# Output projection of a hybrid encoder layer: the second norm one slot later, transposes three tiles behind, attention outputs and denominators loaded two tiles at a time

## The chip, the cores and the metric

One Trainium2 chip (trn2); the kernel is one program on 1 core. The metric is device microseconds of one execution, lower is better. Where the text says "before", it is the kernel ahead of the change.

## The reference, cut to what matters

One encoder layer on x of 2048 positions by 1024 channels, in float32. The part around the change is the end of the mixing sub-layer and the start of the MLP:

```python
attn = dilated_attention(q, k, v, rel_bias).reshape(B, S, D_ATTN)          # 8 heads x 64
sgu = spatial_gating(jax.nn.gelu(zu), jax.nn.gelu(zv), ...)                # 512 channels
mix = jnp.concatenate([attn, sgu], axis=-1) @ w_out                        # (2048 x 1024) @ (1024 x 1024)
x = x + rms_norm(mix, g_post_mix)                                          # first norm
h = rms_norm(x, g_pre_ffn)                                                 # second norm
f = jnp.square(jax.nn.relu(h @ w_ff1)) @ w_ff2                             # hidden width 4096
return x + rms_norm(f, g_post_ffn)
```

The attention output of a head is a sum over three branches divided by a common denominator. The kernel stores the undivided sum and the reciprocal of the denominator, and multiplies the two when the output projection loads them.

## The kernel before, in words

Every matrix product is made of three passes (`mm3`, lines 90 to 94): each float32 operand is split into a high half, rounded to float32r, and the rest, and high times low, low times high and high times high are summed in PSUM. So a product of a 128-position tile with 512 output columns over 128 input channels is three matmuls of 128x512.

The program has three stages. Stage 1 (line 158) makes q, k, v and the gate's inputs. Stage 2 (line 387) does the attention head by head; between its steps a filler, `gate` (line 665), makes the spatial gating unit, and then the half of the output projection that belongs to the gate's 512 channels: its tiles `ot` go to the DRAM tensor `part` (2048 x 1024). The attention sums go to the DRAM tensor `od` (512 channels x 2048 positions) and the reciprocal denominators to `rd` (8 heads x 2048). Stage 3 (line 880) adds the attention half of the projection to `part`, does both norms, and then runs the MLP in two halves of 1024 positions.

The change is in stage 3's first loop (lines 953 to 1025), the output projection. It has 18 slots, `i` = 0 to 17, and works on tiles of 128 positions. In slot `i` before the change:

- `halves(i + 1)` (line 971): ScalarE casts the tile `fa` (attention output, already multiplied) to its high half `mh`, VectorE makes the rest `ml` (lines 59 and 60).
- Loads, all issued from SyncE's queue: `load_x(i)` (the residual, line 963, 3 buffers), `load_part(i + 1)` (line 957, 4 buffers, tile `r`), and `load_attn(i + 3)` (line 863): two DMAs for the denominators `fd`, each broadcasting the rows of 4 heads over 64 partitions, and one for `fa`. `fd` lies in the buffers `g` and `fs` in turn, one buffer each; `fa` in one of three `fr`.
- TensorE: 24 matmuls of 128x512 for the tile, in two halves `n` of 512 columns; in slots 7 to 9 and 11 to 14 also the steps of two early units of the MLP's first product (`early`, line 983; a step is 6 matmuls of 128x512, 16 steps in all; the ninth step of a unit is its end, where ScalarE, GpSimd and VectorE make `sq`, its square and the split `fh`, `fl`, lines 938 to 947).
- The first norm of tile `i - 1`: `meansq` (line 897) is a pass of ScalarE that squares and sums `r` (`jk`), then two small GpSimd instructions give `rs`; VectorE multiplies `r` by `rs` and the gain (line 1009) and adds the residual (line 1010).
- The result is stored to `x1d` by a DMA issued from ScalarE's own queue (line 1012), and for the first 8 tiles the second norm follows at once: `normed` (line 905) is another `meansq` of the same tile and a ScalarE pass that scales it into the residual's buffer `xt` (line 907).
- VectorE adds the PSUM banks `mo` to `r` (line 1016), one for each half.
- `turned(i - 2)` (line 909): 8 TensorE transposes of 128x128, two ScalarE casts `hh`, two VectorE subtractions `hl`.
- `product(i + 2)` (line 875): GpSimd multiplies `fa` by `fd`.
- In slots 1 to 4 two weight pieces `wraw` of the MLP are loaded; in slots 2 to 5 the two of the slot before are split into `wh` and `wl` (lines 56 and 57).

Tile 0's attention load and product stand at the end of stage 2 (lines 855 and 856), tile 1's and 2's loads at the head of stage 3. The order in which these lines stand is the order of execution on each engine: at the end of the loop `in_order` (line 35) chains all instructions of TensorE, ScalarE, VectorE, GpSimd and SyncE in program order. So an instruction that waits holds back all that follows it on its engine, and a DMA that waits for its buffer holds back all later DMAs of its queue.

```python
   985	                if i + 1 < 16:
   986	                    halves(i + 1)
...
  1007	                    if old and n == 0:
  1008	                        rs = meansq(r)
...
  1013	                        if i - 1 < 8:
  1014	                            normed(r, xt)
...
  1017	                if 0 <= i - 2 < 8:
  1018	                    turned(xs[i - 2], h[0], h[1], i - 2)
  1019	                if i + 2 < 16:
  1020	                    product(nc, c, i + 2)
```

Of the kernel before, what the change touches and what calls it, by code (L numbers as in the profile page):

```python
# [9 lines left out]
F32 = mybir.dt.float32  # L10
F32R = mybir.dt.float32r
BF16 = mybir.dt.bfloat16
AF = mybir.ActivationFunctionType
ALU = mybir.AluOpType
# [3 lines left out]
P = 128  # L18
# [3 lines left out]
DH = 64  # L22
# [30 lines left out]
def split_sbuf(nc, src, hi, lo, scale=None):  # L53

    if scale is not None:
        nc.scalar.activation(hi, src, AF.Copy, scale=scale)  # L56
        nc.vector.scalar_tensor_tensor(lo, src, scale, f32(hi), ALU.mult, ALU.subtract)  # L57
        return
    nc.scalar.copy(hi, src)  # L59
    nc.vector.tensor_tensor(lo, src, f32(hi), ALU.subtract)  # L60
# [326 lines left out]
def stage2(tc, c, a):  # L387
    nc = tc.nc
    LEAD = 2
    with ExitStack() as ctx:  # L390
# [386 lines left out]
        for s_ in range(NH * NG):  # L777
            g = s_ % NG
# [73 lines left out]
            for run in jobs.pop(min(jobs)):  # L852
                run()
        c.loads = {}
        load_attn(nc, c, 0)
        product(nc, c, 0)
        for _ in fill:
            pass
# [1 line left out]

def load_attn(nc, c, i):

    sl = slice(i * P, (i + 1) * P)
    fa = c.fk.tile([P, 4, P], F32, name="fa", tag="fr", bufs=3)
    fr = c.fk.tile([P, 512], F32, name="fd", tag=("g", "fs")[i % 2], bufs=1).rearrange("p (k s) -> p k s", k=4)
    rv = c.rd[:, sl].rearrange("(k e) s -> e k s", e=2)
    for e in range(2):
        nc.sync.dma_start(fr[e * DH:(e + 1) * DH], rv[e].partition_broadcast(DH))  # L870
    nc.sync.dma_start(fa, c.od[:, sl].rearrange("(k p) s -> p k s", p=P))
    c.loads[i] = fa, fr


def product(nc, c, i):
    fa, fr = c.loads[i]
    nc.gpsimd.tensor_tensor(fa, fa, fr, ALU.mult)


def stage3(tc, c, a, out):  # L880
    nc = tc.nc
# [3 lines left out]
    with ExitStack() as ctx:  # L885
# [11 lines left out]
        def meansq(src):  # L897
            jk = wk.tile([P, 512], F32, name="jk3", tag="sq").bitcast(BF16)
            ms = sm.tile([P, 1], F32, name="ms3", tag="ms3")
            nc.scalar.activation(jk, src, AF.Square, scale=1.0 / 32.0, accum_out=ms)  # L900
            rs = sm.tile([P, 1], F32, name="rs3", tag="rs3")
            rstd_pow(nc, rs, ms, RMS_EPS, c)
            return rs

        def normed(x1, out):
            rs = meansq(x1)
            nc.scalar.activation(out, x1, AF.Copy, scale=rs)

        def turned(x1, hh, hl, i):
            for j in range(2):  # L910
                t = pt.tile([P, 512], F32, name="tp3", tag="tp3")
                for k in range(4):
                    kc = 4 * j + k
                    nc.tensor.transpose(t[:, k * P:(k + 1) * P], x1[:, kc * P:(kc + 1) * P], c.ident)
                split_psum(nc, t.rearrange("p (k t) -> p k t", k=4), hh[:, 4 * j:4 * j + 4, i * P:(i + 1) * P],
                           hl[:, 4 * j:4 * j + 4, i * P:(i + 1) * P])
# [6 lines left out]
        h = new_h()  # L923
# [29 lines left out]
        with ExitStack() as octx:  # L953
            orp = octx.enter_context(tc.tile_pool(name="s3r", bufs=4, side="right"))
            gmix = bcast_row(nc, cst, a["g_post_mix"][0:1], D, "gmix", "gain")

            def load_part(i):

                r = orp.tile([P, D], F32, name="r", tag="r")
                nc.sync.dma_start(r, c.part[i * P:(i + 1) * P, :])  # L960
                return r

            def load_x(i):
                xt = wk.tile([P, D], F32, name="xt3", tag="xt3", bufs=3)
                nc.sync.dma_start(xt, x2[i * P:(i + 1) * P, :])
                return xt

            start = len(nc.cur_bb.bb.instructions)
            parts, xs, ops = {}, {}, {}

            def halves(i):
                mh = c.fk.tile([P, 4, P], F32R, name="mh", tag="xh", bufs=2)
                ml = c.fk.tile([P, 4, P], F32R, name="ml", tag="xl", bufs=2)
                split_sbuf(nc, c.loads.pop(i)[0], mh, ml)
                ops[i] = mh, ml

            load_attn(nc, c, 1)
            parts[0] = load_part(0)
            halves(0)
            load_attn(nc, c, 2)  # L980
            product(nc, c, 1)
            raws, ws0, fs0, fs1 = [], [], [], []
            early = {7: 3, 8: 3, 9: 3, 11: 3, 12: 2, 13: 2, 14: 2}
            for i in range(18):
                if i + 1 < 16:
                    halves(i + 1)
                if i < 16:
                    xs[i] = load_x(i)
                if i + 1 < 16:
                    parts[i + 1] = load_part(i + 1)  # L990
                if i + 3 < 16:
                    load_attn(nc, c, i + 3)
                if i in (7, 11):
                    unit = ff1_unit(h, ws0, 0, (i // 11,), fs0, fpa)
                old = 0 <= i - 1 < 16
                if old:
                    r, xt = parts[i - 1], xs[i - 1]
                for n in range(2):
                    if i < 16:
                        b = pm.tile([P, 512], F32, name="mo", tag="mm3")  # L1000
                        ns = slice(n * 512, (n + 1) * 512)
                        mh, ml = ops[i]
                        for kc in range(4):
                            mm3(nc, b, mh[:, kc, :], ml[:, kc, :], *c.wo[4 * n + kc], kc == 0, kc == 3)
                    for _ in range((early.get(i, 0) + 1 - n) // 2):
                        next(unit, None)
                    if old and n == 0:
                        rs = meansq(r)
                        nc.vector.scalar_tensor_tensor(r, r, rs, gmix, ALU.mult, ALU.mult)
                        nc.vector.tensor_tensor(r, r, xt, ALU.add)  # L1010
                    if old and n == 1:
                        nc.scalar.dma_start(x1d[(i - 1) // 8][((i - 1) % 8) * P:((i - 1) % 8 + 1) * P, :], r)
                        if i - 1 < 8:
                            normed(r, xt)
                    if i < 16:
                        nc.vector.tensor_tensor(parts[i][:, ns], b, parts[i][:, ns], ALU.add)
                if 0 <= i - 2 < 8:
                    turned(xs[i - 2], h[0], h[1], i - 2)
                if i + 2 < 16:
                    product(nc, c, i + 2)  # L1020
                for _ in range(len(raws)):
                    ws0.append(piece_split(nc, c, raws.pop(0), c.gffn[:, len(ws0):len(ws0) + 1]))
                if 1 <= i < 5:
                    raws = [piece_load(nc, c, w1[kc * P:(kc + 1) * P, 0:512]) for kc in range(2 * i - 2, 2 * i)]
            in_order(tc, start, ("PE", "Activation", "DVE", "Pool", "SP"))
# [194 lines left out]
```

## Time and profile before

| | us |
|---|---|
| three runs | 2499.51, 2507.77, 2511.3 |
| their median | 2507.77 |
| the profiled execution's own time | 2505.61 |
| its span, first to last instruction | 2503.8 |
| TensorE busy in the span | 2391.6 (96%) |
| output projection, first to last `mo` matmul | 954.7 to 1108.8 |

All times in the rows below are microseconds from the start of the span of that one profiled execution, unless marked ns. TensorE (PE) is busy nearly everywhere, but its matmuls are pipelined and a busy TensorE may run at a lower clock: the column PEclk gives the clock that was granted, as a share of 2.4 GHz. DVE is VectorE, ACT ScalarE, POOL GpSimd; SPq and ACTq are the DMA queues of SyncE and ScalarE. "Idle before" an instruction is how long its engine stood idle ahead of it, with what ended the wait.

### The profile page before, as it was taken

What the parts mean: (1) busy time and instruction counts of PE and PEld (TensorE: products, weight loads), DVE (VectorE), ACT (ScalarE), POOL (GpSimd) and SP (SyncE); (2) the same over time, 40 slices, a digit from 0 to 9 for tenths busy, and PEclk for the clock granted to TensorE, in tenths of its full rate; (3) what the DMA queues carried; (4) which work ended last, traced back from release to release, by engine and by line L of the source; (5) the groups of instructions that cost most, each with busy time, mean ns of one, the idle gap of its engine ahead of it and who ended that gap; (6) DMA issues with size and microseconds to landing.
All of it is one profiled execution on the core that took longest, in us unless ns stands there. A gap on an engine that the chain in (4) does not pass through costs nothing.

```text
span 2503.8 us, 31495 instructions
## 1 busy us (share of the span) xinstructions
PE 2391.6 (96%) x11591; PEld 1994.1 (80%) x11591; DVE 1063.0 (42%) x2246; ACT 930.8 (37%) x2053; POOL 459.3 (18%) x521
## 2 busy tenths in 40 slices
PE   7999999989888887999999999999999999999998
PEld 6787888878777776778888888888788888888887
DVE  5534523667766643651323332332722233233326
ACT  4424422467766662523221221123533122212212
POOL 4103103633222222320110010011211001001101
PEclk9999999999899998999999999999999999999999
DMA  7736365877776556872111211111611111111113
GB/s 270 221 134 202 135 187 164 223 183 184 190 184 160 144 156 184 234 242 68 51 51 34 67 46 48 43 51 59 211 51 51 40 62 48 49 39 54 48 47 118
DMA packets 222078, 296.14 MB, mean 118 GB/s; under 512 B 37089, under 2 KB 128740, under 8 KB 218852
## 3 DMA queue, kind: packets, MB, share of 16 engines
q1 hardware_dynamic: 214404, 272.62, 36.8%
q10 hardware_dynamic: 4960, 17.31, 1.8%
q0 software_dynamic: 2560, 4.20, 1.2%
q8 instruction: 91, 1.49, 0.2%
q14 instruction: 63, 0.52, 0.1%
HBM read 216.04 MB, written 82.74 MB: 119 GB/s over the span
## 4 chain that ended last, share of the span: by engine, by line
PE 60%; DMA 9%; DVE 4%; ACT 3%; POOL 2%; issue 1%; SPq 1%; ACTq 0%; DVEq 0%; POOLq 0%
PE f L92 10%; PE f L93 10%; PE f L94 10%; PE g L92 8%; PE g L94 8%; PE g L93 8%; DMA fa<-od 2%; DMA v<-vd 2%; PE t L595 1%; PE o L623 1%; PE o L624 1%; PE s L515 1%; ACT p L584 1%; PE s L516 1%; DMA x1b<-stb 1%
## 5 line engine op out<-in xcount | busy, mean ns | idle before, releaser
L92 PE MATMUL g<-wl,fh 128*128 128x512 f32 x1024 | 399.1, 390 | 0.4 <-ACT sq L945 0.4
L94 PE MATMUL g<-wh,fh 128*128 128x512 f32 x1024 | 398.8, 389 | 0.0
L93 PE MATMUL g<-wh,fl 128*128 128x512 f32 x1024 | 398.7, 389 | 0.0
L94 PE MATMUL f<-hh,wh 128*128 128x512 f32 x1024 | 398.7, 389 | 0.0
L93 PE MATMUL f<-hh,wl 128*128 128x512 f32 x1024 | 398.7, 389 | 0.0
L92 PE MATMUL f<-hl,wh 128*128 128x512 f32 x1024 | 398.5, 389 | 0.0
L946 POOL TENSOR_TENSOR sq<-sq 128x512 f32<-128x512 f32 x128 | 134.0, 1066 | 1150.7 <-ACT sq L945 1150.7
L56 ACT ACTIVATE wh<-wraw,gain 128x512 fp32r<-128x512 f32 x200 | 143.2, 724 | 504.0 <-PE g L94 423.3
L57 DVE SCALAR_TENSOR_TENSOR wl<-wraw,gain,wh 128x512 fp32r<-128x512 f32 x200 | 157.9, 797 | 265.1 <-ACT wh L56 264.4
L60 DVE TENSOR_TENSOR fl<-sq,fh 128x512 fp32r<-128x512 f32 x128 | 100.3, 783 | 383.4 <-ACT fh L59 372.8
L92 PEld LDWEIGHTS g<-wl,fh 128*128 128x128 f32 x1024 | 192.3, 188 | 40.4 <-ACT sq L945 0.8
L93 PEld LDWEIGHTS f<-hh,wl 128*128 128x128 f32 x1024 | 192.2, 188 | 40.1
L92 PEld LDWEIGHTS f<-hl,wh 128*128 128x128 f32 x1024 | 192.2, 188 | 40.1
L94 PEld LDWEIGHTS f<-hh,wh 128*128 128x128 f32 x1024 | 192.2, 188 | 39.9
L94 PEld LDWEIGHTS g<-wh,fh 128*128 128x128 f32 x1024 | 192.2, 188 | 39.8
L93 PEld LDWEIGHTS g<-wh,fl 128*128 128x128 f32 x1024 | 192.3, 188 | 39.6
L1073 DVE TENSOR_TENSOR acc<-g,acc 128x512 f32<-128x512 f32 x192 | 127.2, 687 | 165.1 <-PE g L94 165.1
L584 ACT ACTIVATE p<-p,m 128x256 f32<-128x256 f32 (+2 forms) x384 | 174.1, 459 | 18.8 <-DVE m L556 18.8
L945 ACT ACTIVATE sq<-f 128x512 f32<-128x512 f32 x128 | 74.6, 597 | 281.0 <-PE f L94 274.3
L60 DVE TENSOR_TENSOR wl<-wraw,wh 128x512 fp32r<-128x512 f32 x136 | 93.8, 690 | 165.9 <-ACT wh L59 164.6
L59 ACT CAST wh<-wraw 128x512 fp32r<-128x512 f32 x136 | 84.5, 622 | 183.2 <-PE f L94 162.4
L532 DVE CUSTOM_DVE_ANT_0 p<-s,bias 128x256 f32<-128x256 f32 (+2 forms) x384 | 121.1, 355 | 39.1 <-PE s L516 25.4
(166 smaller groups left out, 4158.5 us busy)
## 6 DMA issues: line engine op xcount, KB each, us to landing
wraw<-in_w_ff_dram SPq DMA_DIRECT2D x256, 256.0 KB, 2.7
wraw<-in_w_in_dram SPq DMA_DIRECT2D x72, 256.0 KB, 2.8
xt<-in_x_dram SPq DMA_DIRECT2D x32, 512.0 KB, 6.6
v<-vd SPq DMA_DIRECT2D x40, 256.0 KB, 6.4
v<-vd SPq DMA_DIRECT2D x8, 1088.0 KB, 7.7
hd<-ht ACTq DMA_DIRECT2D x16, 512.0 KB, 4.6
vd<-vt SPq DMA_DIRECT2D x16, 512.0 KB, 3.3
qd<-e SPq DMA_DIRECT2D x32, 256.0 KB, 2.8
```

Of the source, the lines that this page charges most:

```text
L56: nc.scalar.activation(hi, src, AF.Copy, scale=scale)
L57: nc.vector.scalar_tensor_tensor(lo, src, scale, f32(hi), ALU.mult, ALU.subtract)
L59: nc.scalar.copy(hi, src)
L60: nc.vector.tensor_tensor(lo, src, f32(hi), ALU.subtract)
L92: nc.tensor.matmul(out, lhsT=lh, rhs=rl, start=start, stop=False)
L93: nc.tensor.matmul(out, lhsT=ll, rhs=rh, start=False, stop=False)
L94: nc.tensor.matmul(out, lhsT=lh, rhs=rh, start=False, stop=stop)
L532: nc.vector.tensor_tensor_reduce(po, so, bo, -1.0, 1e38, ALU.add, ALU.min, o.nm[:, br, cc:cc + 1])
L584: nc.scalar.activation(p[:, at + lo:at + hi], p[:, at + lo:at + hi], AF.Exp, bias=o.m[:, br, cc:cc + 1], scale=-1.0, accum_out=o.dn[:, br, ...
L945: nc.scalar.activation(sq, bs[k * len(es) + e], AF.Relu)
L946: nc.gpsimd.tensor_tensor(sq, sq, sq, ALU.mult)
L1073: nc.vector.tensor_tensor(av, b, av, ALU.add)
```

## The change

- The second norm of a tile moves one slot later: in slot `i` `meansq` runs for tile `i - 2` (second norm) and then for tile `i - 1` (first norm), both ahead of the slot's matmuls in program order; the scaling into `xt` is for tile `i - 2`.
- The store to `x1d` moves to the next slot and from ScalarE's queue to SyncE's, at the head of the slot's loads.
- `turned` works on tile `i - 3` and moves from the end of the slot to its start, ahead of the tile's matmuls.
- `load_attn` loads two tiles (256 positions) at once, in even slots. It is cut by channels instead: for each half of the channels (4 heads) two denominator DMAs and one of the outputs, so that `fa` and `fd` are two tiles of 128x512 each. The numbers and sizes of the DMAs for two tiles stay (4 of 128 KB and 2 of 256 KB), their contiguous pieces grow from 512 B to 1 KB. `fd` lies in `g` and `fs`, both used by each pair; the first pair's lie in stage 2's pool `p`. `fa` lies in `fr`, for odd pairs the second half in `fu`.
- `product` multiplies both halves of a pair, in even slots; the load of the next pair stands right behind it. `halves` splits a tile in two pieces of 128x256.

```diff
@@ -852,7 +852,7 @@
             for run in jobs.pop(min(jobs)):
                 run()
         c.loads = {}
-        load_attn(nc, c, 0)
+        load_attn(nc, c, 0, pp)
         product(nc, c, 0)
         for _ in fill:
             pass
@@ -860,21 +860,26 @@
 
 
 
-def load_attn(nc, c, i):
-
-    sl = slice(i * P, (i + 1) * P)
-    fa = c.fk.tile([P, 4, P], F32, name="fa", tag="fr", bufs=3)
-    fr = c.fk.tile([P, 512], F32, name="fd", tag=("g", "fs")[i % 2], bufs=1).rearrange("p (k s) -> p k s", k=4)
-    rv = c.rd[:, sl].rearrange("(k e) s -> e k s", e=2)
-    for e in range(2):
-        nc.sync.dma_start(fr[e * DH:(e + 1) * DH], rv[e].partition_broadcast(DH))
-    nc.sync.dma_start(fa, c.od[:, sl].rearrange("(k p) s -> p k s", p=P))
-    c.loads[i] = fa, fr
+def load_attn(nc, c, i, pool=None):
+
+    sl = slice(2 * i * P, 2 * i * P + 2 * P)
+    fa, fd = [], []
+    for j in range(2):
+        fa.append(c.fk.tile([P, 512], F32, name="fa", tag=("fr", ("fr", "fu")[i % 2])[j],
+                            bufs=(3, (3, 1)[i % 2])[j]).rearrange("p (k s) -> p k s", k=2))
+        d = pool.tile([P, 512], F32, name="fd", tag="p") if pool else \
+            c.fk.tile([P, 512], F32, name="fd", tag=("g", "fs")[j], bufs=1)
+        fd.append(d.rearrange("p (k s) -> p k s", k=2))
+        rv = c.rd[4 * j:4 * j + 4, sl].rearrange("(k e) s -> e k s", e=2)
+        for e in range(2):
+            nc.sync.dma_start(fd[j][e * DH:(e + 1) * DH], rv[e].partition_broadcast(DH))
+        nc.sync.dma_start(fa[j], c.od[2 * j * P:2 * j * P + 2 * P, sl].rearrange("(k p) s -> p k s", p=P))
+    c.loads[i] = fa, fd
 
 
 def product(nc, c, i):
-    fa, fr = c.loads[i]
-    nc.gpsimd.tensor_tensor(fa, fa, fr, ALU.mult)
+    for fa, fd in zip(*c.loads[i]):
+        nc.gpsimd.tensor_tensor(fa, fa, fd, ALU.mult)
 
 
 def stage3(tc, c, a, out):
@@ -971,30 +976,33 @@
             def halves(i):
                 mh = c.fk.tile([P, 4, P], F32R, name="mh", tag="xh", bufs=2)
                 ml = c.fk.tile([P, 4, P], F32R, name="ml", tag="xl", bufs=2)
-                split_sbuf(nc, c.loads.pop(i)[0], mh, ml)
+                for j, fa in enumerate(c.loads[i // 2][0]):
+                    split_sbuf(nc, fa[:, :, i % 2 * P:i % 2 * P + P], mh[:, 2 * j:2 * j + 2, :], ml[:, 2 * j:2 * j + 2, :])
                 ops[i] = mh, ml
 
             load_attn(nc, c, 1)
             parts[0] = load_part(0)
             halves(0)
-            load_attn(nc, c, 2)
-            product(nc, c, 1)
             raws, ws0, fs0, fs1 = [], [], [], []
             early = {7: 3, 8: 3, 9: 3, 11: 3, 12: 2, 13: 2, 14: 2}
             for i in range(18):
+                old = 0 <= i - 1 < 16
+                if 0 <= i - 3 < 8:
+                    turned(xs[i - 3], h[0], h[1], i - 3)
                 if i + 1 < 16:
                     halves(i + 1)
+                if 0 <= i - 2 < 16:
+                    nc.sync.dma_start(x1d[(i - 2) // 8][((i - 2) % 8) * P:((i - 2) % 8 + 1) * P, :], parts[i - 2])
+                    if i - 2 < 8:
+                        rs2 = meansq(parts[i - 2])
+                if old:
+                    rs = meansq(parts[i - 1])
                 if i < 16:
                     xs[i] = load_x(i)
                 if i + 1 < 16:
                     parts[i + 1] = load_part(i + 1)
-                if i + 3 < 16:
-                    load_attn(nc, c, i + 3)
                 if i in (7, 11):
                     unit = ff1_unit(h, ws0, 0, (i // 11,), fs0, fpa)
-                old = 0 <= i - 1 < 16
-                if old:
-                    r, xt = parts[i - 1], xs[i - 1]
                 for n in range(2):
                     if i < 16:
                         b = pm.tile([P, 512], F32, name="mo", tag="mm3")
@@ -1005,19 +1013,17 @@
                     for _ in range((early.get(i, 0) + 1 - n) // 2):
                         next(unit, None)
                     if old and n == 0:
-                        rs = meansq(r)
+                        r = parts[i - 1]
                         nc.vector.scalar_tensor_tensor(r, r, rs, gmix, ALU.mult, ALU.mult)
-                        nc.vector.tensor_tensor(r, r, xt, ALU.add)
-                    if old and n == 1:
-                        nc.scalar.dma_start(x1d[(i - 1) // 8][((i - 1) % 8) * P:((i - 1) % 8 + 1) * P, :], r)
-                        if i - 1 < 8:
-                            normed(r, xt)
+                        nc.vector.tensor_tensor(r, r, xs[i - 1], ALU.add)
+                    if 0 <= i - 2 < 8 and n == 1:
+                        nc.scalar.activation(xs[i - 2], parts[i - 2], AF.Copy, scale=rs2)
                     if i < 16:
                         nc.vector.tensor_tensor(parts[i][:, ns], b, parts[i][:, ns], ALU.add)
-                if 0 <= i - 2 < 8:
-                    turned(xs[i - 2], h[0], h[1], i - 2)
-                if i + 2 < 16:
-                    product(nc, c, i + 2)
+                if i % 2 == 0 and i + 2 < 16:
+                    product(nc, c, i // 2 + 1)
+                    if i + 4 < 16:
+                        load_attn(nc, c, i // 2 + 2)
                 for _ in range(len(raws)):
                     ws0.append(piece_split(nc, c, raws.pop(0), c.gffn[:, len(ws0):len(ws0) + 1]))
                 if 1 <= i < 5:
```

## Rows read from the trace of the kernel before

**Rows 1.** Windows: PE, PEld, DVE, ACT, POOL busy us, PEclk, DMA share, GB/s

```profile
960.00:970.00 10.00, 2.03 (x6) 1.07 (x5) 1.56 (x3) 0.62 (x1) 1.26 (x1) 0.63 0.84 174
970.00:1028.00 58.00, 48.42 (x182) 36.41 (x181) 31.84 (x42) 28.54 (x47) 15.45 (x26) 0.83 0.78 231
1006.00:1017.00 11.00, 8.67 (x33) 6.35 (x32) 6.94 (x11) 6.07 (x11) 2.83 (x5) 0.84 0.69 218
1028.00:1058.00 30.00, 29.24 (x135) 23.75 (x135) 17.57 (x23) 15.17 (x26) 8.54 (x15) 1.00 0.87 250
1072.00:1109.00 37.00, 37.00 (x162) 30.18 (x161) 19.59 (x22) 8.83 (x16) 10.95 (x14) 1.00 0.70 232
```

**Rows 2.** TensorE's waits, 954 to 1122: us in total, times, longest us

```profile
PE mo L92 <- ACT mh L59: 9.7, 5, 8.0
PE mo L93 <- DVE ml L60: 3.1, 4, 1.8
PE tp L914 <- DVE hl L84: 6.3, 4, 3.2
PE tp L914 <- ACT xt L907: 1.8, 1, 1.8
```

**Rows 3.** Timeline of SyncE's queue and of GpSimd: start, us, instruction, idle before

```profile
956.96 0.57 SPq L871 DMA_DIRECT2D fa<-od  x1
...
966.50 1.26 POOL L877 TENSOR_TENSOR fa<-fa,fd 128x512 f32<-128x512 f32 x1 [15.64 <-DMA fa<-od]
```

**Rows 4.** Timeline of ScalarE, slots 1 to 6

```profile
974.66 0.62 ACT L59 CAST mh<-fa 128x512 fp32r<-128x512 f32 x1 [6.25 <-POOL fa L877]
...
1005.67 0.61 ACT L59 CAST mh<-fa 128x512 fp32r<-128x512 f32 x1
...
1011.27 1.06 ACT L900 ACTIVATE jk<-r 128x1024 bf16<-128x1024 f32 x1 [3.94 <-DVE r L1010]
...
1013.42 1.15 ACT L907 ACTIVATE xt<-r,rs 128x1024 f32<-128x1024 f32 x1 [0.99 <-POOL rs L99]
...
1027.63 0.61 ACT L59 CAST mh<-fa 128x512 fp32r<-128x512 f32 x1
```

**Rows 5.** Timeline of TensorE: tile 0, then transposes and tile 7

```profile
957.83 0.39 PE L93 MATMUL mo<-qs,ml 128*128 128x512 f32 x1
...
960.10 0.39 PE L94 MATMUL mo<-ks,mh 128*128 128x512 f32 x1
...
1026.80 1.25 PE L914 MATMUL tp<-ident,xt 128*128 128x128 f32 x8 [0.32 <-DVE hl L84]
1028.30 0.51 PE L92 MATMUL mo<-qs,mh 128*128 128x512 f32 x1 [0.25 <-ACT mh L59]
```

**Rows 6.** VectorE's groups by shape, 880 to 1130: busy us, mean ns, idle before

```profile
L60 DVE TENSOR_TENSOR ml<-fa,mh 128x512 fp32r<-128x512 f32 x16 | 11.0, 687 | 46.3 <-ACT mh L59 46.3
```

**Rows 7.** DMA queues and issues, 954 to 1037: KB each, median us to landing

```profile
q1 hardware_dynamic: 12853, 14.94, 66.2%
q10 hardware_dynamic: 833, 3.05, 9.1%
...
r<-part SPq DMA_DIRECT2D x9, 512.0 KB, 7.4
xt<-in_x_dram SPq DMA_DIRECT2D x8, 512.0 KB, 13.0
x1d<-r ACTq DMA_DIRECT2D x6, 512.0 KB, 9.6
fd<-rd SPq DMA_DIRECT2D x18, 128.0 KB, 11.9
...
wraw<-in_w_ff_dram SPq DMA_DIRECT2D x9, 256.0 KB, 10.1
```

**Rows 8.** Timeline of ScalarE in slot 9, end of the first early unit

```profile
1058.51 0.59 ACT L945 ACTIVATE sq<-f 128x512 f32<-128x512 f32 x1
...
1063.85 0.63 ACT L59 CAST fh<-sq 128x512 fp32r<-128x512 f32 x1 [2.12 <-POOL sq L946]
```

## The prediction

> **What bounds the kernel now.** I read the page first, where TensorE is busy nearly throughout, so only stretches in which it waits or runs slow can give time. The windows show where the change's stretch is of that kind: from 960 to 970 it works 2.03 of 10 us at a clock of 0.63, from 970 to 1028 it works 48.42 of 58 us at 0.83, and from 1072 to 1109 it works 37.00 of 37 at full clock [rows 1]. So the output projection loses time in its first seven tiles and next to none later, where the early MLP steps fill TensorE. How much there is to win: the waits of TensorE in the stretch add up to 9.7 + 3.1 + 6.3 + 1.8 = 20.9 us [rows 2], and the lower clock costs about 2.03 x 0.37 + 48.42 x 0.17 = 9.0 us [rows 1]. The ceiling is some 30 us, 1.2% of the time. A difference under 0.5% (12.5 us) can't be told from none here.
>
> What it waits for is read from two timelines. The longest wait is tile 1: GpSimd stood idle 15.64 us before its product at 966.50, because `fa` was issued only at 956.96 [rows 3]. After it each slot is paced by ScalarE. In slot 4 it casts `mh` at 1005.67, squares tile 3, and then, at 1011.27, it has stood idle 3.94 us before the second square of the same tile, which needs VectorE's multiply and add, and 0.99 us for the root [rows 4]; `mh` of slots 1 and 6 stand at 974.66 and 1027.63, so five slots take 53.0 us, 10.6 each. The scaled `xt`, the transposes and the next slot's `mh` all queue behind that. TensorE sees the end of it.
>
> **The change, part by part.** All is summed against the profiled execution, 2505.61 us (span 2503.8).
>
> *First stall.* Pair 0 brings tiles 0 and 1 in stage 2. Its first half of channels needs heads 0 to 3 only, which are long done; the second half lands when tile 0's load lands now. So tile 1 needs no load in this stage. A tile is 24 matmuls; ten steps from 957.83 to 960.10 give 0.227 us each [rows 5], 5.45 us a tile. Tile 0 ends at 960.33, so it began at 954.9, and tiles 0 and 1 end at 965.8. Tile 2 needs pair 1, whose second half must wait for the buffers `fs` and `fu` that stage 2's last output tiles use, so it is issued at about the time of the `fa` of [rows 3]. That one took 966.50 - 956.96 = 9.5 us to land, but for tile 1; pair 1 has 2 more product pieces behind it and half of it comes earlier. Bounds for tile 2's start: 965.8 (no wait) and 970 (966.5, the product's 1.26 us, a cast, a subtraction and as much again for the second half). I take 968.
>
> *The slot, engine by engine.* The two idle times of ScalarE, 3.94 and 0.99 us, go: the second square is for a tile finished in the slot before. What is late next is a resource, so I add up each.
> - TensorE: 5.45 us for the tile and 8 transposes in at most 1.25 us [rows 5]: 6.7. They now stand ahead of the tile's matmuls, but use an `xt` scaled in the slot before.
> - ScalarE: busy 6.07 of 11.00 us in the window of slot 4 [rows 1]. The cast in two pieces of 128x256 adds a little: one piece costs between 0.31 and 0.61 us (half and whole of the cast of 128x512 [rows 4]); I take 0.40, nearer the half, since the piece's length is what is halved, so +0.2: 6.3.
> - VectorE: busy 6.94 [rows 1]; two subtractions in place of one of 687 ns [rows 6], between 0.34 and 0.69 each, 0.42 by the same choice: +0.15. That is 7.1.
> - GpSimd keeps its instructions; 2.83 [rows 1] is far from the bound.
> - The store of `x1d` leaves ScalarE's queue for SyncE's: the same DMA. On SyncE it waits for VectorE's add of the slot before, which is over by then; behind it stand the slot's `x`, `part` and pair loads. The buffer of `part` comes free a slot later, but a slot is still in hand.
> - DMA: a share of 0.78 from 970 to 1028 [rows 1] is 0.78 x 10.6 = 8.3 us of all sixteen engines in a slot. So the engines can't go much faster than now unless transfers get cheaper. The store queue shows the price of 4 KB rows: 3.05 MB in 0.091 x 83 = 7.55 us, 404 GB/s [rows 7]. SyncE's queue is busy 0.662 x 83 = 54.9 us; its 9 `part`, 8 `x`, 9 `wraw` and one `ot` are 11.5 MB, 28.5 us at that rate; the rest, 26.4 us, is 9 tiles of `fa` and `fd`, 2.9 us a tile of 1024 pieces, 45 ns a piece on one engine. At 404 GB/s 512 B would be 20 ns, so 25 ns are fixed. 512 pieces of 1 KB then cost 25 + 40 = 65 ns each, 2.1 us a tile: 0.8 saved. Bounds: 1.45 (cost by piece) and 0 (cost by byte). 8.3 - 0.8 = 7.5.
>
> The Trainium skill, in "DMA: Bandwidth & Descriptors", section "Specifications", puts the least transfer for line rate at 512 B. By it the old pieces were already at full rate and nothing is saved; the 45 ns worked out from [rows 7], against 20, do not agree. That outcome is the first rival.
>
> DMA is the largest, and it doesn't run without gaps: the busiest whole stretch shows 0.87 [rows 1]. I take 0.9, so a slot of 8.3 us where it was 10.6. Five slots (tiles 2 to 6): 968 + 41.5 = 1009.5 for tile 7, which began at 1028.30 [rows 5]: 18.8 us earlier.
>
> *What is given back.* Slots 7 to 15 are bound by TensorE in both kernels, so the lead is kept, with one exception. In slot 9 ScalarE ends the early unit from 1058.51 to 1064.5 (last `fh` at 1063.85, 0.63 us) [rows 8]. The scaling of tile 7 now stands behind it (before, it was a slot earlier), and `turned(7)` stands ahead of tile 10's matmuls. From the start of TensorE's slot 9: transposes and first half of the tile and two steps of 6 matmuls, about 1.1 + 2.7 + 2.7 = 6.5 us to `sq`; 6 us to the last `fh`; 1.15 to scale: 13.7. TensorE ends slot 9 after 6.5 + 2.7 = 9.2. It stands about 4.4 us. Tile 11's wait for `ml` at that place (1.8 us, the longest of its row [rows 2]) goes instead: 2.6 us lost net.
>
> Sum: 2505.6 - 18.8 + 2.6 = 2489.4. The three runs' median, 2507.77, is 2.2 above the profiled execution; I add part of that: **2490 us**.
>
> **The rivals.**
> 1. *Pieces of 1 KB are no cheaper*, as the skill's line of 512 B would have it. For it: from 960 to 970 the engines are busy 0.84 at only 174 GB/s [rows 1], which could be the place of the reads and not their size. Then a slot is 8.3 / 0.9 = 9.2 us, tile 7 starts at 968 + 46 = 1014, and the gain is 14.3 - 2.6 = 11.7: 2494, with its own bad end near 2500.
> 2. *The pair's load in series with its product.* `g` and `fs` now serve every pair, so the next pair's load can't be issued before the product of this one, and that product waits for its landing. Six issues like the 0.57 us of [rows 3] take 3.4 us, landing 11.9 (median of `fd`) to 13.0 (`x`, the slowest) [rows 7], two products of 1.26 another 2.5: 17.8 to 18.9 us for two slots, 8.9 to 9.45 a slot. Against it: loads ahead in the queue get shorter too. Tile 7 then starts at 1012.5 to 1015.3, and slots 11 to 15, which TensorE holds at 7.6 us (five tiles of 5.45 and 8 early steps of 6 matmuls in five slots), stretch by 5 x 1.3 to 1.85. Gain 13.0 to 15.8, less 2.6 and 6.5 to 9.3: 2499 to 2504, the same within what can be told.
> 3. *Slower: one queue, waits in series.* SyncE now holds the store, the wait of `part` for the landing of the store before last (9.6 us median [rows 7]) and the pair's wait for the product. If these add up instead of running side by side, two slots cost 9.6 + 17.8 = 27.4 us, 13.7 a slot, and it lasts to tile 15: 968 + 14 x 13.7 = 1160 against 1109 now, full to the end of the last window of [rows 1]: 2557. It decides from an average slot of (1109 - 968) / 14 = 10.1 us. Against it: a store is issued a slot before the load that waits for it.
>
> **How the numbers follow.** My forecast 0.60 (its own range 2482 to 2494: tile 2 at 965.8 and slots of 7.3, just over VectorE's 7.1, to tile 2 at 970 and slots of 8.8), rival 1 0.15, rival 2 0.12, rival 3 0.10; 0.03 for more than the sum. The range for 8 in 10 reaches from 2480 to 2504: below by the 0.03's nearest part, above through rival 1's bad end and most of rival 2. Faster by over 0.5% (under 2495): 0.57 of the forecast's 0.60, 0.06 of rival 1 and the 0.03: 0.66. Within 0.5%: 0.03 of the forecast, 0.09 of rival 1, 0.11 of rival 2: 0.23. Slower: rival 3 and 0.01 of rival 2: 0.11.
>
> **What would show it.** Right: product of tile 1 before 953 and no wait of TensorE at tile 1; ScalarE's idle before the second square gone; `mh` of successive slots 8 to 8.5 us apart; tile 7's first matmul near 1010; a wait of `tp` for `xt` of some 4 us at the head of slot 10; a DMA share near 0.9 with more GB/s than the 231 of [rows 1]. Wrong: `mh` 9 us or more apart with GpSimd waiting for `fa` or `fd` (rivals 1 and 2, told apart by the DMA share: high in 1, low in 2); SyncE's queue waiting in turn for `x1d` and for the product (rival 3); TensorE waiting for transposes in every slot.

## The result and the profile after

The changed kernel took 2486.82 us (median of five runs, 2482.68 to 2488.97) against 2508.55 (five, 2499.51 to 2513.37): a ratio of 0.9916, 95% interval 0.9899 to 0.9932. Forecast were 2490, with a range of 2480 to 2504. The profiled execution took 2488.97 us.

From the start of the first `mo` matmul to the start of the last one it is 141.6 us, before 153.5 ("the projection" from here on); from there to the end 1394.4, before 1395.4. The profiled span is 16.6 us shorter: 11.9 in the projection, 1.0 behind it, and 3.7 because the projection began earlier (951.2 against 954.9). The last is not counted as an effect: in the 14 profiles of this study the projection begins between 951.0 and 960.7, with no order by kernel. A second profile of the kernel before has 156.8 us of projection, so in one pair of profiles 12 to 15 us of the medians' 21.7 have a place. The rest was not placed.

Three views of the changed kernel answer to [rows 1], [rows 2] and [rows 4]: the windows, TensorE's waits from 950 to 1125, and ScalarE's waits from 950 to 1025 (us in total, times, longest).

```profile
960.00:970.00 10.00, 8.01 (x35) 5.97 (x33) 6.33 (x10) 4.81 (x10) 2.10 (x6) 1.00 0.95 212
970.00:1020.00 50.00, 40.17 (x160) 32.69 (x161) 39.31 (x49) 30.78 (x54) 19.75 (x27) 0.83 0.82 271
1055.00:1090.00 35.00, 35.00 (x154) 28.49 (x153) 23.20 (x29) 9.55 (x20) 8.94 (x13) 1.00 0.71 249
```

```profile
PE tp L919 <- ACT xt L1020: 14.0, 5, 3.7
PE mo L93 <- DVE ml L60: 0.2, 1, 0.2
```

```profile
ACT wh L56 <- DMA wraw<-in_w_ff_dram: 14.2, 4, 5.7
```

From 960 to 970 TensorE works 8.01 us where it worked 2.03, now at full clock (2.4 GHz): the first stall is gone. From 970 to 1020 little is better, the granted clock of 0.83 included, and the waits have a new name. TensorE waits for the scaled `xt`, and ScalarE, which scales it, waits for the weight pieces `wraw` of the early MLP steps. SyncE's queue, ScalarE, TensorE and GpSimd show the rest, in their timelines (start, us, instruction, idle before).

```profile
955.37 0.38 SPq L876 DMA_DIRECT2D fa<-od  x1
...
971.71 1.24 SPq L875 DMA_DIRECT2D fd<-rd  x2
973.32 0.38 SPq L876 DMA_DIRECT2D fa<-od  x1
974.00 1.56 SPq L875 DMA_DIRECT2D fd<-rd  x2
976.30 0.69 SPq L876 DMA_DIRECT2D fa<-od  x1
977.80 2.37 SPq L70 DMA_DIRECT2D wraw<-in_w_ff_dram  x2
```

```profile
977.17 1.07 ACT L905 ACTIVATE jk<-r 128x1024 bf16<-128x1024 f32 x1
...
978.23 1.05 ACT L905 ACTIVATE jk<-r 128x1024 bf16<-128x1024 f32 x1
...
979.50 1.15 ACT L1020 ACTIVATE xt<-r,rs 128x1024 f32<-128x1024 f32 x1
986.37 1.36 ACT L56 ACTIVATE wh<-wraw,gain 128x512 fp32r<-128x512 f32 x2 [5.73 <-DMA wraw<-in_w_ff_dram]
```

```profile
962.12 0.39 PE L92 MATMUL mo<-qs,mh 128*128 128x512 f32 x1
962.70 0.50 PE L93 MATMUL mo<-qs,ml 128*128 128x512 f32 x1 [0.20 <-DVE ml L60]
...
1013.43 0.78 PE L92 MATMUL mo<-qs,mh 128*128 128x512 f32 x1
...
1046.50 1.33 PE L919 MATMUL tp<-ident,xt 128*128 128x128 f32 x5 [2.39 <-ACT xt L1020]
```

```profile
958.52 1.29 POOL L882 TENSOR_TENSOR fa<-fa,fd 128x512 f32<-128x512 f32 x1 [11.58 <-DMA fa<-od]
```

The two squares follow each other without idle time, as the change is meant to bring. Then ScalarE stands 5.73 us for a weight piece: the two pieces were issued at 977.80, behind the pair's six loads (1 MB), and all that follows on ScalarE, the cast `mh` of the next tile included, stands behind the split. Tile 2 starts at 962.12 and tile 7 at 1013.43: 51.3 us for five slots, **10.3 each**. In the kernel before, the same count gives 21.4 us after tile 0 for tile 2 and 73.4 for tile 7 (its row stands in [rows 5]): 10.4 each. So of the 11.2 us by which tile 7 comes earlier, 10.5 were there at tile 2; the slots, on which the prediction rested most, gave 0.7.

### The profile page after: what moved, and what is told of

It reads as the page before. It is cut to its first block, busy times and chain, and to the rows that moved or that the text cites. A ratio compares the mean times of both kernels' runs of the same rounds, so it can differ in the third digit from the quotient of the medians.

```text
span 2487.2 us, 31523 instructions
## 1 busy us (share of the span) xinstructions
PE 2383.5 (96%) x11591; PEld 1992.6 (80%) x11591; DVE 1072.9 (43%) x2262; ACT 933.7 (38%) x2069; POOL 462.3 (19%) x521
## 4 chain that ended last, share of the span: by engine, by line
PE 63%; DMA 7%; DVE 4%; ACT 3%; issue 1%; POOL 1%; SPq 1%; ACTq 0%; DVEq 0%; POOLq 0%
PE f L93 10%; PE f L92 10%; PE f L94 10%; PE g L93 8%; PE g L92 8%; PE g L94 8%; DMA v<-vd 2%; PE t L595 1%; PE o L623 1%; PE o L624 1%; ACT p L584 1%; DMA x1b<-stb 1%; PE s L515 1%; PE s L516 1%; DMA yd<-x1b 1%
## 5 line engine op out<-in xcount | busy, mean ns | idle before, releaser
L584 ACT ACTIVATE p<-p,m 128x256 f32<-128x256 f32 (+2 forms) x384 | 174.1, 459 | 20.7 <-DVE m L556 20.7
```

The source lines that it names most:

```text
L584: nc.scalar.activation(p[:, at + lo:at + hi], p[:, at + lo:at + hi], AF.Exp, bias=o.m[:, br, cc:cc + 1], scale=-1.0, accum_out=o.dn[:, br, ...
```

## The experiments

A tile's start is counted in every trace as here: the first of its 24 `mo` matmuls, from tile 0's. "Slots 2 to 6" is the mean from tile 2's start to tile 7's; single slots differ much from it. Times of different runs are best compared by their ratios, since the kernel before was timed anew beside each group of runs (medians of 2508.55 to 2513.5 us).

| kernel | ratio to before, interval | tile 2 at | slots 2 to 6 | projection |
|---|---|---|---|---|
| before | | 21.4 | 10.4 | 153.5 |
| after | 0.9916 (0.9899 to 0.9932) | 10.9 | 10.3 | 141.6 |
| e1 pairs only | 0.9925 (0.991 to 0.9939) | 10.9 | 11.0 | 147.3 |
| e2 norm only | 0.9983 (0.997 to 0.9997) | 20.9 | 10.5 | 152.3 |
| e3 pieces spread | 0.9876 (0.9859 to 0.9893) | 10.9 | 8.4 | 129.7 |
| e4 one piece | 0.9884 (0.9865 to 0.9902) | 10.9 | 8.2 | 130.4 |
| e5 512 B | 0.9995 (0.9981 to 1.0009) | 10.9 | 13.4 | 158.9 |
| e6 store from ScalarE | 0.9938 (0.9922 to 0.9953) | 10.9 | 11.1 | 143.7 |
| e9 split later | 0.9872 (0.9859 to 0.9885) | 10.9 | 8.1 | 126.0 |
| e10 = e9, 512 B | 0.9938 (0.9923 to 0.9953) | 10.9 | 10.3 | 142.6 |
| e11 = e9, part first | 0.9855 (0.9836 to 0.9874) | 10.9 | 8.1 | 125.7 |
| e12 = e9, product early | 0.9869 (0.9847 to 0.989) | 10.9 | 8.9 | 129.6 |
| e13 = e1, pieces as e9 | 0.9934 (0.992 to 0.9948) | 10.9 | 10.5 | 146.7 |

**The two parts alone.** e1 keeps the pair loads and undoes the rest; e2 keeps the rest, with `load_attn` by tile as before.

```diff
 e1, against after (in the slot):
-                    turned(xs[i - 3], h[0], h[1], i - 3)
...
+                        rs = meansq(r)
...
+                        nc.scalar.dma_start(x1d[...], r)
+                        if i - 1 < 8:
+                            normed(r, xt)
...
+                    turned(xs[i - 2], h[0], h[1], i - 2)
 e2, against after:
-    sl = slice(2 * i * P, 2 * i * P + 2 * P)
+    sl = slice(i * P, (i + 1) * P)
```

> The kernel before with the pair loads alone; both norms, the store and the transposes stay where they were. Theory A (the pair loads give the gain, by the first stall of 8 us and its low clock; the later norm gains little because ScalarE's split of the weight pieces now waits for a DMA): tile 0's first matmul to tile 2's is 11 us instead of 20, slots 2 to 6 stay at 10.5 us or more, time 8 to 13 us under before, ratio 0.995 to 0.997. Theory B (the later norm gives the gain, as my prediction's slot of 8.3 us had it): at most 9 us of the 22 come from here and the ratio is 0.9965 or more. Told apart from each other by this run together with the next.

> The changed kernel with the loads of before: one tile at a time, three tiles ahead. The order of norms, store and transposes is the changed one. Theory A: the first stall of 8 us stays; the weight pieces queue behind loads of one tile, half as long, so ScalarE's wait for them is under half of the 14.2 us it has in the changed kernel, and slots 2 to 6 take 9 to 9.5 us; time 5 to 8 us under before, ratio 0.997 to 0.998. Theory B: slots of 8 to 8.5 us, 12 us or more under before, ratio 0.995 or less.

e1 took 2497.22 us and e2 2508.44. Pairs alone take the first stall away (tile 2 at 10.9), but their slots are no shorter; the norms alone gain 0.2%, and there TensorE's first stall stays at 7.8 us. The interval of e1 overlaps that of the changed kernel, so in time the norms' share of the gain is not clear of noise.

ScalarE's waits for weight pieces over the projection, in e1 and then in e2:

```profile
ACT wh L56 <- DMA wraw<-in_w_ff_dram: 0.7, 2, 0.4
```

```profile
ACT wh L56 <- DMA wraw<-in_w_ff_dram: 15.2, 4, 5.1
```

In e1 the pieces stand behind the pair's 1 MB and hardly anyone waits; in e2 they stand behind the 512 KB of one tile, as before the change, and the wait is as long as the 14.2 us of the changed kernel. So the wait does not come from the larger load ahead in the queue. It comes with the new norm order: without its idle time of 3.94 and 0.99 us a slot ScalarE reaches the split that much earlier, ahead of the landing.

**The size of the pieces.** e5 cuts a pair by tile and not by channels: as many loads, buffers and bytes, but pieces of 512 B (and the split of a tile is one instruction again, which speaks for e5 if anything).

```diff
-    sl = slice(2 * i * P, 2 * i * P + 2 * P)
...
+        sl = slice((2 * i + j) * P, (2 * i + j + 1) * P)
...
-        rv = c.rd[4 * j:4 * j + 4, sl].rearrange("(k e) s -> e k s", e=2)
+        rv = c.rd[:, sl].rearrange("(k e) s -> e k s", e=2)
...
-        nc.sync.dma_start(fa[j], c.od[2 * j * P:2 * j * P + 2 * P, sl].rearrange("(k p) s -> p k s", p=P))
+        nc.sync.dma_start(fa[j], c.od[:, sl].rearrange("(k p) s -> p k s", p=P))
```

> The changed kernel with the same pair loads, buffers, places and number of DMAs (4 of 128 KB, 2 of 256 KB for two tiles), but cut by tile and not by channels, so that the contiguous pieces are 512 B as before and not 1 KB; the split is one instruction again. Prediction's estimate: 0.8 us of all DMA engines a tile, and up to 1.45: the landing of the pairs is later, slots 2 to 6 slower by 0.5 to 1.5 us each, 4 to 9 us above the changed kernel, ratio to before 0.993 to 0.995. Prediction's rival 1 (pieces of 1 KB are no cheaper): as the changed kernel, 0.991 to 0.992.

2512.59 us: the whole gain is gone, with the first stall still removed. ScalarE's waits and TensorE's, over the projection:

```profile
ACT wh L56 <- DMA wraw<-in_w_ff_dram: 25.8, 3, 9.5
```

```profile
PE tp L919 <- ACT xt L1019: 25.4, 5, 8.8
```

The wait for the weight pieces has grown from 14.2 us to 25.8. Whether the small pieces cost by themselves, or only through this wait, is not told apart here; e10 bears on that.

**The weight pieces.** e3 loads one piece a slot, ahead of the pair load; e4 loads a single piece and splits all eight from it. e4 leaves out seven of these loads, so the early steps multiply by that one piece throughout, and its time holds 1.8 MB less of transfers.

```diff
 e3:
+                if i < 8:
+                    raws.append(piece_load(nc, c, w1[i * P:(i + 1) * P, 0:512]))
...
-                for _ in range(len(raws)):
+                if 1 <= i < 9:
                     ws0.append(piece_split(...))
-                if 1 <= i < 5:
-                    raws = [piece_load(...) for kc in range(2 * i - 2, 2 * i)]
```

> The changed kernel with the eight weight pieces of the MLP loaded one in each of slots 0 to 7, ahead of the pair's load in SyncE's queue, and split in the slot after, where it was two in slots 1 to 4 behind the pair's load. Same bytes. Theory A (the wait of ScalarE's split for a piece queued behind the pair's load is what holds slots 2 to 6 at 10.3 us): the wait falls from 14.2 us to under 3, TensorE's wait for xt from 14.0 to under 6, tile 7 starts 52 to 56 us after tile 0 instead of 62.2; 6 to 10 us under the changed kernel, ratio to before 0.988 to 0.989. Theory C (the DMA engines are full, so the place in the queue only says who waits): TensorE's waits stay above 10 us and the ratio is 0.991 to 0.993.

> The changed kernel with one weight piece loaded in slot 0 and all eight splits made from it: seven loads of 256 KB are left out, so the first MLP weights are wrong ones; every split, matmul and other load stays. Theory A: as the run before it, tile 7 starts 51 to 55 us after tile 0, and the two runs differ by less than 3 us, ratio 0.987 to 0.989. Theory C: seven pieces are 1.8 MB, 4.5 us of the DMA engines at 404 GB/s, so 3 to 5 us under the changed kernel and clearly under the run before it.

2483.46 and 2484.49 us, slots of 8.4 and 8.2 on the mean, near the 8.3 of the prediction. In e3 ScalarE still waits 20.9 us for pieces in all, but in eight waits, each at the end of a slot; the DMA share is 0.91 at 273 GB/s over the first 55 us of the projection. A sum of waits alone told nothing; the place of the wait did. The means hide unlike slots, though: in e3 slots 2 to 6 last 9.8, 11.1, 8.2, 6.4 and 6.4 us, and in the last two TensorE is busy throughout (12.70 of 12.70 us). And e4, with 1.8 MB less to move, is no faster than e3.

**The late split, and each cause put back into it.** e9 is e3 with each piece split two slots after its load and the scaling of tile i - 2 ahead of the early steps. e13 puts the old norm order back (e1 with e9's weight pieces), e10 the pieces of 512 B (e5's edit).

```diff
 e9, against e3:
+                    if 0 <= i - 2 < 8 and n == 0:
+                        nc.scalar.activation(xs[i - 2], parts[i - 2], AF.Copy, scale=rs2)
                     for _ in range((early.get(i, 0) + 1 - n) // 2):
...
-                if 1 <= i < 9:
+                for _ in range((0, 0, 1, 1, 1, 1, 1, 1, 2)[i] if i < 9 else 0):
```

> The kernel with the weight pieces spread over slots 0 to 7 ahead of the pair's load, and two more changes: each piece is split two slots after its load instead of one (the last two in slot 8), and the scaling of tile i - 2 stands ahead of the early unit's end, not behind. ScalarE still waited 20.9 us for pieces in the spread kernel, one slot after their issue. Theory A: that wait falls under 3 us, TensorE's waits for xt (8.9 us there) under 3, tile 7 starts 46 to 50 us after tile 0 (52.8 there, 62.2 in the changed kernel); 3 to 7 us under the spread kernel, ratio 0.985 to 0.987. Theory C (DMA bound from here on): the wait only moves to ScalarE's casts or VectorE's adds, and the ratio stays at 0.9875.

> Setting: the version with the weight pieces ahead of the pair load and split two slots after their load, scaling of tile i-2 ahead of the early unit's end (it measured 2482.3, 0.9872), and one edit: the pairs cut by tile, so pieces of 512 bytes in as many loads of the same size. In the changed kernel itself that edit cost 25.8 us, with ScalarE waiting 25.8 us for weight pieces. Theory A (the smaller pieces only make the queue slower, and the cost came from ScalarE's wait for weight pieces, which hardly exists here): below 0.990, at most some 6 us above that version, TensorE's waits under 12 us. Theory B (the pieces cost by themselves, whatever waits for them): the product waits for fd or fa in the even slots, the ratio is 0.993 or higher, 15 us or more above. The prediction's own price, 0.8 us a tile with bounds 0 and 1.45, would be 4 to 9 us over the 6 to 8 tiles in question, between the two.

> Pair loads alone, with norms, store, scaling and transposes where they were before, and the weight pieces as in the version with the late split: one load in each of slots 0 to 7 ahead of the pair load, split two slots later. Here neither the loads nor the weight pieces should hold a slot, so it shows whether the norm order is worth anything once they don't. Theory A (the norm order takes the 3.94 us of ScalarE's idle out of each of the slots 2 to 6, as the prediction had it, and was only hidden behind the weight pieces in the changed kernel): the idle before the second square is back at 3 to 4 us, slots 2 to 6 last 9 us or more, and the time is 8 to 16 us above the late-split version, 0.991 to 0.994. Theory B (the pair loads and the weight pieces were all that held the slots): within 4 us of the late-split version, 0.986 to 0.989.

e9 took 2482.3 us, and TensorE's wait for `xt` is down to 4.3 us. e13 took 2496.62: its slots are back at 10.5, and ScalarE's timeline shows why, the idle time of [rows 4] to the hundredth.

```profile
986.64 1.06 ACT L905 ACTIVATE jk<-r 128x1024 bf16<-128x1024 f32 x1
...
991.74 1.06 ACT L905 ACTIVATE jk<-r 128x1024 bf16<-128x1024 f32 x1 [3.94 <-DVE r L1014]
...
993.88 1.15 ACT L912 ACTIVATE xt<-r,rs 128x1024 f32<-128x1024 f32 x1 [0.99 <-POOL rs L99]
```

So two things held these slots at nearly the same length: the norm's chain at 10.5 (e13) and the split of the weight pieces at 10.3 (the changed kernel). Taking away either leaves the other; with both gone the mean is 8.1 (e9). e13 puts norms, store and transposes back together, so the difference is that of the three; and of the 20.7 us by which its projection is longer than e9's, 11.8 lie in slots 2 to 6 and 8.7 in slots 8 and 9, where TensorE waits 5.4 us for weight splits.

What bounds a slot when both are gone is not settled. From tile 3 to tile 7, in e9 and then in e11 (described below; TensorE, its weight loads, VectorE, ScalarE, GpSimd, then clock, DMA share, GB/s):

```profile
977.60:1008.30 30.70, 28.66 (x130) 23.14 (x129) 27.03 (x37) 23.01 (x41) 15.87 (x21) 0.90 0.96 296
```

```profile
974.70:1003.40 28.70, 27.66 (x131) 22.62 (x129) 28.05 (x37) 22.79 (x41) 14.55 (x20) 0.93 0.89 302
```

In e9 the DMA engines are the fullest, in e11 VectorE is (28.05 of 28.70 us), with TensorE close behind in both.

e10 took 2496.44, 14 us above e9 (0.7% by the ratios). Its projection is 16.6 us longer: 8.8 in slots 2 and 3 (13.6 and 13.0 us for 10.0 and 7.8), 1.9 in slots 4 to 6, and 5.9 behind tile 7, nearly all in slot 9, ahead of which ScalarE waits 8.85 us for the last weight piece. Up to tile 7 there is hardly a wait for weight pieces, so there the small pieces cost by themselves. The DMA views of e9, then of e10, from 970 to 1020 (packets, bytes and sizes; then SyncE's queue and its share of 16 engines), each under its window row:

```profile
970.00:1020.00 50.00, 45.59 (x209) 36.99 (x208) 42.11 (x56) 34.40 (x60) 22.67 (x31) 0.93 0.93 282
```

```profile
DMA packets 7140, 14.11 MB, mean 282 GB/s; under 512 B 697, under 2 KB 4192, under 8 KB 7136
...
q1 hardware_dynamic: 7136, 14.07, 93.0%
```

```profile
970.00:1020.00 50.00, 42.17 (x176) 33.99 (x176) 33.40 (x38) 28.68 (x48) 19.29 (x28) 0.85 0.91 238
```

```profile
DMA packets 8965, 11.88 MB, mean 238 GB/s; under 512 B 584, under 2 KB 6515, under 8 KB 8963
...
q1 hardware_dynamic: 8963, 11.85, 90.4%
```

The engines are as busy in both and move 16% less in e10. Worked out as the prediction did: e9 has 4192 - 697 = 3495 pieces of 1 KB, 3.58 MB; the other 10.49 MB take 26.0 us at the 404 GB/s of [rows 7]; of the queue's 46.5 us (0.930 x 50) 20.5 are left, 94 ns a piece on one engine. e10 has 5931 pieces of 512 B: 45.2 - 21.8 = 23.4 us, 63 ns a piece. A tile costs 512 x 94 / 16 = 3.0 us or 1024 x 63 / 16 = 4.0: **1.0 us saved a tile**, an estimate, since all that is unlike large transfers is put on the small pieces. The traces' records of single packets in the same stretch give a mean of 85 ns for the 3495 and 55 ns for the 5931, 0.8 us a tile; their medians are 46 and 27 ns, so slow pieces among them make up much of the price. Slots 4 to 6 differ by about as much (7.6 and 8.3 on the mean), the mean of all five by more (8.1 and 10.3): from 960 to 1030 VectorE's two lines that wait for `x` and `part` do so 24.8 us in e10, 14.0 in e9.

**Three smaller questions.** e6 issues the store of `x1d` from ScalarE's queue; e11 has `part` and `x` of tile 0 loaded ahead of pair 1; e12 has product and pair load right behind the cast.

```diff
 e6, against after:
-                    nc.sync.dma_start(x1d[...], parts[i - 2])
+                    nc.scalar.dma_start(x1d[...], parts[i - 2])
 e11, against e9:
-            load_attn(nc, c, 1)
             parts[0] = load_part(0)
+            xs[0] = load_x(0)
+            load_attn(nc, c, 1)
 e12, against e9 (taken from the slot's end):
+                if i % 2 == 0 and i + 2 < 16:
+                    product(nc, c, i // 2 + 1)
+                    if i + 4 < 16:
+                        load_attn(nc, c, i // 2 + 2)
```

> The changed kernel with the store of the first norm's result issued from ScalarE's queue again, at the same place of the slot. If the move to SyncE's queue matters (the store waits there for VectorE and holds back the slot's loads, 33.1 us of such waits in the trace of the changed kernel), the loads come earlier and the time is 3 us or more under the changed kernel, ratio below 0.990. If those waits only stand where SyncE would have waited for a buffer or a product anyway, the time is within 2 us of the changed kernel, 0.991 to 0.993; ScalarE pays 0.33 us a slot for the issue.

> Setting: the same version, with the loads of part(0) and x(0) put ahead of pair 1's load in SyncE's queue before the loop. Theory: tile 2's and tile 3's slots are late because VectorE's first add waits for part(0), which stands behind the pair's loads (VectorE waited 7.9 us for it in the changed kernel); with part first, tile 3 starts 2 to 4 us earlier relative to tile 0 and the time is 1 to 4 us less, 0.986 or so. Rival: pair 1's landing then becomes late by as much, and tile 2 waits for it: no change, or tile 2 later by 1 to 3 us.

> Setting: the same version, with the product of the next pair and the load behind it issued in even slots right behind the cast of the next tile, ahead of the norms. Theory: in the changed kernel VectorE's two adds of the norm take 2.29 and 2.19 us in slots in which GpSimd's product runs beside them, against 1.28 and 1.22 alone; with the product earlier these adds are short again in even slots, the loads start 2 to 3 us earlier, and the loop loses 2 to 4 us: 0.986. Rival: the product then overlaps the split's subtraction and the sum of mo instead and these grow by as much, or GpSimd waits for the pair's landing with nothing won: within 2 us of that version.

e6 (2498.56 us) has longer slots, 11.1: taking the store off SyncE's queue gains nothing. It came out above both of the outcomes put on record; why it is slower was not followed up. e11 (2474.65) and e12 (2477.75) can't be told from e9 by their intervals. In e11 the projection lasts 125.7 us against 126.0, and its tile 3 starts at 22.7 rather than 20.9: what `part` won, pair 1 lost, the rival's outcome. e12's 129.6 us bring nothing either: its slot 2 lasts 14.9 us for 10.0 in e9, and slots 3 to 6 are 0.3 us shorter on the mean.

> The kernel before once more, for a second profile: from the first to the last matmul of the projection the first profile has 153.5 us, and the sums of what the four experiments save there are 7 to 12 us short of what their times save. If the first profile is a lucky one of before, this stretch is 158 us or more here; if it is 152 to 155 again, the rest of the savings lies outside the stretch, in what varies from run to run.

The kernel before, profiled again, took 2509.73 us; its projection lasted 156.8.

## Why the prediction was right, and where it was wrong

- **Direction and size**: right, 2486.82 for 2490. That the profile's sum, 2489.4, meets 2488.97 is luck: the projection gave 11.9 of the 16.2 forecast, and within it the parts are not the forecast ones. 4.7 us of the pair of profiles lie outside the projection.
- **First stall**: right, and under-sized; it is nearly all of the gain (10.5 us of 11.2 at tile 7). Tile 2 was put at 13.1 us after tile 0 and came at 10.9, waiting 0.20 us. The step taken from [rows 3], 9.5 us for the second half to land, was too long: `fa` was issued at 955.37 and its product stood at 958.52.
- **ScalarE's idle of 3.94 and 0.99 us**: right in mechanism. It went (977.17, 978.23, 979.50 above), but gave 0.7 us over five slots. Once nothing hides it, it is worth some 12 us in these slots, with store and transposes (e13 against e9).
- **"What is late next is a resource"**: this step failed. The sum of engines gave 8.3 us a slot, and 10.3 were measured. Next was a wait, ScalarE's split for weight pieces: the prediction counted their bytes, but not that ScalarE, rid of 4.9 us of idle time a slot, comes to the split before they have landed (5.73 us at 986.37; e2 against e1), and that `mh` of the next tile stands behind the split. With that wait moved (e3) the mean slot is 8.4. This doesn't confirm the sum: single slots go down to 6.4, with TensorE busy throughout, and in e11 slots 3 to 6 take 7.2 each with VectorE nearly full (28.05 of 28.70 us) and a DMA share of 0.89.
- **Pieces of 1 KB**: right, 0.8 to 1.0 us a tile for the 0.8 taken (bounds 0 to 1.45), both prices higher than forecast (94 and 63 ns, or 85 and 55, for 65 and 45). But the effect on the time was far beyond that sum: the 512 B of e5 cost 0.8% by the ratios, and those of e10 0.7%, mostly in slots 2 and 3 and in waits for weight pieces. The first rival falls with e5 and e10. By the Trainium skill, "DMA: Bandwidth & Descriptors", section "Specifications", 512 B suffices for line rate; the 238 GB/s of e10 against e9's 282 at nearly the same share (0.91 and 0.93) disagree.
- **Pair load in series with its product** (second rival): its outcome came (a slot over 9 us), its cause did not. Slots of 8.1 with the same buffers (e9) exclude it as the bound.
- **SyncE's queue in series** (third rival): fell. Its slots were 13.7 us, 10.3 were measured, and without the store in that queue (e6) nothing is gained.
- **The stall of slot 10**: right in place, 2.39 us at 1046.50 for the 4.4 forecast. From tile 7 to the last `mo` matmul the changed kernel takes 79.4 us and the one before 80.1, so nothing net was given back where 2.6 was forecast.

## What to carry to other kernels

When an idle time is taken out of an engine that runs in program order, don't go straight to the resources: list what the engine holds next and ask whether its data will have landed when the engine comes there earlier. Here 4.9 us of idle time a slot came back as waits for weight pieces, 14.2 us in four waits of up to 5.7, and all that stood behind the split waited with it. Two waits of nearly the same length hide each other; an order that gains 0.2% alone (e2) can be worth 0.6% once the other wait is gone (e13 to e9). And a mean over unlike slots that meets a forecast does not confirm its mechanism.

## What was not expected of the hardware

The product of a pair, two instructions of GpSimd, ran beside VectorE's two norm steps in every other slot, and both grew. VectorE's timeline, a slot without and a slot with the product, and GpSimd's:

```profile
980.46 1.28 DVE L1017 SCALAR_TENSOR_TENSOR r<-r,rs,gmix 128x1024 f32<-128x1024 f32 x1 [1.09 <-POOL rs L99]
981.77 1.22 DVE L1018 TENSOR_TENSOR r<-r,xt 128x1024 f32<-128x1024 f32 x1
...
992.38 2.29 DVE L1017 SCALAR_TENSOR_TENSOR r<-r,rs,gmix 128x1024 f32<-128x1024 f32 x1 [1.97 <-POOL rs L99]
994.71 2.19 DVE L1018 TENSOR_TENSOR r<-r,xt 128x1024 f32<-128x1024 f32 x1
```

```profile
992.32 3.50 POOL L882 TENSOR_TENSOR fa<-fa,fd 128x512 f32<-128x512 f32 x2
```

Alone the four take 1.28 + 1.22 + 2 x 1.29 = 5.1 us; together they end after 4.6 us (992.32 to 996.90), nearly as if one waited for the other in turn. The Trainium skill, "SBUF — State Buffer", section "Who interferes with whom", says that a VectorE instruction with two inputs in SBUF contends with a GpSimd instruction that reads it; the rows agree. Whether these 2 us of VectorE cost time is not shown. e12 was meant to move them, but there the product runs beside the norm steps of the slot before (981.71, beside 2.31 us at 981.78 and 2.19 at 984.12).
